# A list scheduler's table of durations and latencies, set from a trace, for a hybrid encoder block

## Chip, cores and metric

One core of a Trainium2 chip runs the whole kernel in one launch. The metric is device time in microseconds of one execution. Engines are named as in the profile: PE (TensorE matmul) and PEld (its weight loads), DVE (VectorE), ACT (ScalarE), POOL (GpSimd), SP (SyncE, which here only issues DMAs).

## What is computed

One layer of an encoder block on x of 1024 positions by 1024 channels, all in float32, cut to its main lines:

```python
h = rms_norm(x, g_mix)
glu_a, glu_b, q, k, v, z, a_in, b_in, gate_a, gate_b = split_cols(h @ w_in, IN_SIZES)
c = depthwise_conv(glu_a * sigmoid(glu_b), conv_dw_w) + conv_dw_b          # 31 taps
y_conv = silu(layer_norm(c, conv_ln_g, conv_ln_b)) @ w_conv_out
q, k, v = split(silu(depthwise_conv([q, k, v], qkv_conv_w)))               # 5 taps
q, k = l2_norm(q) * HEAD_DIM ** -0.5, l2_norm(k)                           # 8 heads of 128
o = gated_delta_rule(q, k, v, g_fwd, beta_fwd) \
    + rev(gated_delta_rule(rev(q), rev(k), rev(v), rev(g_bwd), rev(beta_bwd)))
y_delta = (rms_norm(o, delta_norm_g) * silu(z)) @ w_delta_out
x = x + (sigmoid(gate_a) * y_conv + sigmoid(gate_b) * y_delta) @ w_o
x = x + (silu(gt) * up) @ w_down            # gt, up = split(rms_norm(x, g_ffn) @ w_gate_up)
x = x + sigmoid(rms_norm(x, g_pl) @ w_pl_gate) * rms_norm(p @ w_pl_proj, g_pl_proj)
return rms_norm(x, g_final)
```

The gated delta rule is a recurrence over positions, done in chunks: per chunk a unit lower triangular system is solved, then a chain of small matmuls carries a 128x128 state from chunk to chunk, once forward and once backward.

## The kernel before

**Recorded, then ordered.** The functions in `hybrid_block` do not issue instructions. Each calls a method of the class `Plan` (`matmul`, `transpose`, `act`, `tt`, `stt`, `dma`, ...), which appends an operation with its engine, its tiles and a cost in microseconds. `Plan.order` (line 337) then walks through a modelled time. At each step the engine that is free first takes, of the operations whose inputs are ready and for whose new tiles a buffer is free, the one with the lowest level (a priority by section, in `LV`). An operation ends at its start plus its cost, and one that depends on it on another engine is ready `LAT` later. A DMA takes its issue cost on SP, then at least `DMA_LAT`, then its bytes at `DMA_RATE`, one after the other. `SWITCH` is added where ACT needs another function table. `Plan.run` (line 505) issues everything in the order of the modelled starts. Each engine runs its own instructions in exactly that order and waits on semaphores for the others, so the table of costs decides nothing but the order.

**Products.** A float32 matrix is split into a high and a low part in the type fp32r (`split`: a cast on ACT, a subtraction on DVE), and each product is three matmuls (`mm3`: high by high, high by low, low by high) of 128x128 weights by 512 columns. Some large products use a seven-product scheme for 2x2 blocks. Weights are loaded in pieces of 256 KB into `raw` tiles and split into `w` tiles just before use. The kernel uses eight PSUM tiles of 512 columns, named `ps`.

**Stages.** At the start eight tiles of x are loaded (`big`, 512 KB each), squared and summed on ACT, scaled, transposed on PE and split into `hT`; beside that x itself is transposed and spilled, and eight small vectors are loaded into one tile and transposed. Then the input projection runs block by block (`do_qkv`, `do_glu`, `do_z`, `do_gate`), with the depthwise convolutions as `scalar_tensor_tensor` taps of 128x1024 on DVE. In between, as soon as a pair of heads has its q, k and v, the delta-rule sections run (`group`, `head`): d.np builds the chunk matrices, d.inv and d.lev invert them, d.chain is the recurrence, d.out combines the two directions and normalises. After the last projections come the layer norm and the conv projection (cout), the delta projection (dout), w_o, the feed-forward part and the per-layer embedding.

**Two places in a head.** In d.lev (line 1122 on) the inverses of 32x32 blocks are copied into the tiles `eu` and `et` by 32 copies of 32x128 elements on ACT, then two rounds of matmul, negation of the PSUM bank on ACT (`neg`, into an `m2` tile, shown as `m`) and matmul follow. In d.out two banks of matmuls are added to `o` on DVE; ACT squares eight pieces with a running sum (`sso`); DVE forms the mean square (`rn`, three tiny operations), POOL raises it to the power -1/2, DVE multiplies (`m<-big,rn`), and PE transposes the product:

```python
pn.pow(rn, rn, mhalf16[:, :NJ])
for q4 in range(2):
    on = m2()
    pn.tt(on, o[:, js], rn[:, js, None].spread(4, P), ALU.mult)
    for i in range(4):
        pn.transpose(ps[:, cs(i)], on[:, i], ident)
```

In the profile one line stands for all operations of one helper: L239 matmuls, L244 transposes, L261 plain copies and casts on ACT, L268 other ACT functions, L284 DVE, L312 the power on POOL, L332 DMAs.

## Time and profile before

| what | us |
|---|---|
| median of 3 timed runs | 2121.04 (2121.02 to 2121.16) |
| the profiled execution | 2120.64 |
| its span, first to last instruction | 2118.9 |
| mean granted clock of TensorE | 0.993 |
| data moved by DMA | 292.85 MB, 138 GB/s on the mean |

The profile is of one execution. "Busy" is the time that an engine's own instructions cover; a wait is put down to the instruction whose semaphore came last. PE's matmuls are pipelined, so its busy time tells where it is fed, not that it is at its peak. An instruction in float32 proper (the delta-rule sections, the transposes aside) stands in the trace as two matmul records; one in fp32r has one.

### The profile page before, as it was taken

How to read it: one execution, taken by the hardware profiler on the slowest of the kernel's cores; microseconds unless marked ns; L12 is line 12 of the kernel's file. 1: busy time of each engine (PE TensorE's matmuls, PEld its weight loads, DVE VectorE, ACT ScalarE, POOL GpSimd, SP SyncE). 2: the span in 40 equal slices, each digit the busy share in tenths (PEclk: the TensorE clock that was granted, in tenths of full speed). 3: DMA queues.
4: the chain of work that ended last, by engine and by line, in shares of the span. 5: the costliest groups of instructions: out<-in, count | busy, mean ns of one | idle time of the engine just before them, and what ended most of it. 6: DMA issues, size and time to landing. Idle time of an engine off the chain costs nothing.

```text
span 2118.9 us, 29685 instructions
## 1 busy us (share of the span) xinstructions
PE 2068.0 (98%) x10326; PEld 1714.5 (81%) x10326; DVE 1650.1 (78%) x2696; ACT 1137.0 (54%) x2590; POOL 130.4 (6%) x203
## 2 busy tenths in 40 slices
PE   7999999999999999999999999999999999999998
PEld 5888788878888788878888888888888888777888
DVE  4488999977899989888587977797666657888776
ACT  6636656756657655857886445443333335443542
POOL 1000201110110101111100000000000000000000
PEclk9999999999999999999999999999999999999999
DMA  6334224522323412636468587433323337442253
GB/s 216 106 120 133 80 82 140 185 84 80 128 93 124 149 60 78 211 95 204 153 201 253 185 271 245 144 112 113 100 90 109 100 96 258 153 159 86 63 164 107
DMA packets 296726, 292.85 MB, mean 138 GB/s; under 512 B 17945, under 2 KB 217810, under 8 KB 296576
## 3 DMA queue, kind: packets, MB, share of 16 engines
q1 hardware_dynamic: 296576, 290.95, 42.8%
q8 instruction: 81, 1.33, 0.3%
q14 instruction: 69, 0.57, 0.1%
HBM read 205.10 MB, written 85.79 MB: 137 GB/s over the span
## 4 chain that ended last, share of the span: by engine, by line
PE 84%; ACT 7%; DVE 5%; DMA 2%; issue 1%; SPq 0%; DVEq 0%; POOLq 0%; POOL 0%; ACTq 0%
PE ps L239 82%; ACT big L261 4%; DVE big L284 3%; PE ps L244 2%; DVE mid L284 1%; ACT big L268 1%; ACT m L268 1%; DMA big<-in_x_dram 1%; DVE w L284 1%; ACT w L261 1%; DMA big<-d 1%; DMA d<-mid 0%; SPq L332 0%; ACT mid L268 0%; ACT L268 0%
## 5 line engine op out<-in xcount | busy, mean ns | idle before, releaser
L239 PE MATMUL ps<-big,w 128*128 128x512 f32 (+1 forms) x7416 | 1823.7, 399 | 2.9 <-ACT w L261 1.4
L239 PEld LDWEIGHTS ps<-big,w 128*128 128x128 f32 x7416 | 1362.0, 189 | 303.4 <-ACT w L261 2.4
L284 DVE SCALAR_TENSOR_TENSOR big<-big,cw 128x1024 f32<-128x1024 f32 x336 | 434.3, 1299 | 17.3 <-ACT big L268 12.3
L261 ACT CAST w<-raw 128x512 fp32r<-128x512 f32 (+2 forms) x308 | 184.6, 605 | 274.2 <-PE ps L239 216.0
L284 DVE TENSOR_TENSOR w<-raw,w 128x512 fp32r<-128x512 f32 (+2 forms) x308 | 208.2, 682 | 74.4 <-ACT w L261 72.6
L261 ACT CAST w<-mid 128x512 fp32r<-128x512 f32 (+1 forms) x185 | 107.4, 586 | 166.2 <-PE ps L239 104.5
L284 DVE TENSOR_TENSOR big<-big 128x512 fp32r<-128x512 f32 (+2 forms) x222 | 149.5, 702 | 11.0 <-ACT big L261 7.9
L284 DVE TENSOR_TENSOR w<-mid,w 128x512 fp32r<-128x512 f32 (+1 forms) x185 | 118.4, 644 | 44.8 <-ACT w L261 44.0
L284 DVE TENSOR_TENSOR big<-ps,big 128x512 f32<-128x512 f32 (+1 forms) x146 | 100.3, 688 | 43.1 <-PE ps L239 33.2
L239 PEld LDWEIGHTS ps<-big 128*128 128x128 f32 x784 | 101.9, 195 | 15.7 <-issue 8.8
L239 PE MATMUL ps<-big 128*128 128x128 f32 (+1 forms) x784 | 107.1, 283 | 7.3 <-ACT big L261 5.1
L261 ACT COPY big<-big 32x128 f32<-32x128 f32 (+1 forms) x264 | 102.6, 440 | 16.5 <-DVE big L284 12.6
L261 ACT CAST big<-big 128x512 fp32r<-128x512 f32 x147 | 85.8, 619 | 40.6 <-DVE big L284 24.0
L261 ACT COPY big<-ps 32x128 f32<-32x128 f32 (+3 forms) x162 | 66.8, 413 | 62.2 <-PE ps L239 53.1
L261 ACT COPY mid<-ps 128x512 f32<-128x512 f32 x81 | 47.0, 588 | 70.2 <-PE ps L239 57.4
L244 PE MATMUL ps<-ident,big 128*128 128x128 f32 (+1 forms) x432 | 71.5, 279 | 12.8 <-DMA big<-in_x_dram 8.8
L239 PEld LDWEIGHTS ps<-S,big 128*128 128x128 f32 x448 | 71.8, 190 | 10.0 <-DVE S L284 0.2
L239 PE MATMUL ps<-S,big 128*128 128x128 f32 x448 | 75.0, 275 | 0.0
L239 PEld LDWEIGHTS ps<-big,m 128*128 128x128 f32 x512 | 63.8, 194 | 12.2 <-ACT m L268 9.4
L244 PEld LDWEIGHTS ps<-ident,big 128*128 128x128 f32 (+1 forms) x432 | 53.6, 146 | 23.9 <-issue 12.1
L239 PE MATMUL ps<-big,m 128*128 128x128 f32 x512 | 65.7, 279 | 6.4 <-ACT m L268 6.3
L268 ACT ACTIVATE mid<-mid 128x512 f32<-128x512 f32 (+2 forms) x87 | 50.2, 580 | 37.7 <-DVE mid L284 23.7
(161 smaller groups left out, 1714.7 us busy)
## 6 DMA issues: line engine op xcount, KB each, us to landing
raw<-in_w_in_dram SPq DMA_DIRECT2D x128, 256.0 KB, 3.1
d<-mid SPq DMA_DIRECT2D x120, 256.0 KB, 3.0
mid<-d SPq DMA_DIRECT2D x120, 256.0 KB, 3.2
big<-d SPq DMA_DIRECT2D x119, 256.0 KB, 5.1
d<-big SPq DMA_DIRECT2D x103, 256.0 KB, 2.8
big<-dqkv SPq DMA_DIRECT2D x32, 512.0 KB, 5.1
raw<-in_w_gate_up_dram SPq DMA_DIRECT2D x50, 256.0 KB, 3.1
dqkv<-big SPq DMA_DIRECT2D x24, 512.0 KB, 2.8
```

The lines of the kernel that those rows point to most:

```text
L239: o = self.add("pe", lambda: self.nc.tensor.matmul(out.ap(), lhsT.ap(), rhs.ap(), start=start, stop=stop, **kw), [out], [lhsT, rhs], cost)
L244: self.add("pe", lambda: self.nc.tensor.transpose(out.ap(), in_.ap(), ident.ap()), [out], [in_, ident], 0.107)
L261: return self.nc.scalar.copy(out.ap(), in_.ap())
L268: return self.nc.scalar.activation(out.ap(), in_.ap(), func, **kw)
L284: return getattr(e, name)(**{k: v.ap() if isinstance(v, View) else v for k, v in kw.items()})
```

## The change

The table of costs and latencies that `Plan.order` uses is replaced. No operation is added, removed or changed, and every dependence stays. The core of the diff:

```diff
-SWITCH = 2.0
+SWITCH = 1.42
...
-DMA_LAT, DMA_RATE = 1.6, 300000.0
+DMA_LAT, DMA_RATE = (1.95, 1.1), 300000.0
+
+COLD = 15.0
...
-LAT = {("pe", "act"): 0.20, ("pe", "dve"): 0.20, ("act", "pe"): 0.27, ("act", "dve"): 0.14, ("dve", "pe"): 0.26,
...
+LAT = {("pe", "act"): 0.235, ("pe", "dve"): 0.205, ("act", "pe"): 0.16, ("act", "dve"): 0.13, ("dve", "pe"): 0.18,
...
-            cost = max(0.107, n / 2400 + 0.003)
+            cost = max(0.119, n / 2208 + 0.004)
...
-        cost = (0.051 if in_.buf.pool.space == PSUM else 0.093) + in_.n / 1200
+        ps, rows = in_.buf.pool.space == PSUM, out.p1 - out.p0
+        cost = (0.06 if ps else 0.1) + in_.n / (1200 if out.dims[-1][0] < 16 else 600)
+        if rows < P and out.buf.tag == "big" and in_.n <= 256:
+            cost += 0.16 if not ps else 0.115 if rows == 32 else 0.07
...
-                 [out], [in0, in1], 0.3 + out.n * 0.165)
+                 [out], [in0, in1], 0.5 if out.n == 1 else 1.1 if out.n == 4 else 1.7)
...
+            if e == "pe" and now < COLD:
+                o.cost *= 2
```

`DMA_LAT` is now a pair (loads, stores); matmuls and transposes on PE count double in the first 15 us of the modelled time. Other rows of the table (DVE, its 32x32 transpose, POOL's fill and select, the issue cost of a DMA, the remaining latencies) change in the same manner. Eleven lines are added in all, so in the new file L239 is L243, L244 is L248, L261 is L268, L268 is L275, L284 is L291 and L332 is L340.

What that moves, at two places. First SP's queue at the start, from the first tile of x on: `big<-in_x` is a tile of x, `raw` a piece of a weight, `mid` a small vector, `bc` a row of constants. Before:

```order
L332 DMA big<-in_x_dram 128x1024 x4
L332 DMA raw<-in_w_in_dram 128x4x128
L332 DMA bc<-in_dt_bias_dram 128x16
L332 DMA raw<-in_w_in_dram 128x4x128
L332 DMA mid<-in_conv_dw_b_dram 8x128
L332 DMA mid<-in_conv_ln_g_dram 8x128
L332 DMA mid<-in_conv_ln_b_dram 8x128
L332 DMA mid<-in_g_ffn_dram 8x128
L332 DMA mid<-in_g_pl_dram 8x128
L332 DMA mid<-in_g_pl_proj_dram 8x128
L332 DMA mid<-in_delta_norm_g_dram 1x128
L332 DMA raw<-in_w_in_dram 128x4x128 x2
```

And now, from the same place:

```order
L340 DMA big<-in_x_dram 128x1024 x2
L340 DMA raw<-in_w_in_dram 128x4x128
L340 DMA bc<-in_dt_bias_dram 128x16
L340 DMA raw<-in_w_in_dram 128x4x128
L340 DMA mid<-in_conv_dw_b_dram 8x128
L340 DMA mid<-in_conv_ln_g_dram 8x128
L340 DMA mid<-in_conv_ln_b_dram 8x128
L340 DMA mid<-in_g_ffn_dram 8x128
L340 DMA mid<-in_g_pl_dram 8x128
L340 DMA mid<-in_g_pl_proj_dram 8x128
L340 DMA mid<-in_delta_norm_g_dram 1x128
L340 DMA big<-in_x_dram 128x1024 x2
```

The third and fourth tile of x moved from the front to behind two weight pieces, a row of constants and seven vectors.

Second, the d.out of the third head (near 550 us in the trace of before). On ACT, where `COPY big<-big 32x4x32` are the copies into `eu` and `et` of the next head's d.lev and `m_...,sso` the eight squares; before:

```order
L261 COPY big<-big 32x4x32 x10
L268 ACTIVATE m_4642,sso<-big 128x128
L261 COPY big<-big 32x4x32
L268 ACTIVATE m_4642,sso<-big 128x128 x2
L261 CAST w<-raw 128x512 x2
L268 ACTIVATE m_4642,sso<-big 128x128
L268 ACTIVATE m_4722,sso<-big 128x128 x4
L261 COPY big<-big 32x4x32 x12
```

And now:

```order
L268 COPY big<-big 32x4x32 x3
L275 ACTIVATE m_4698,sso<-big 128x128
L268 COPY big<-big 32x4x32
L275 ACTIVATE m_4698,sso<-big 128x128 x3
L268 COPY big<-big 32x4x32
L275 ACTIVATE m_4775,sso<-big 128x128 x4
L268 COPY big<-big 32x4x32 x12
```

Seven copies left the place ahead of the first square, and two casts of weights the place between the squares, which one more copy took.

On DVE in the same d.out, where the two `big<-ps,big` are the sums onto `o` and `SCALAR_TENSOR_TENSOR big<-big,cw` are convolution taps; before:

```order
L284 TENSOR_TENSOR big<-ps,big 128x512
L284 SCALAR_TENSOR_TENSOR big<-big,cw_606 128x1024
L284 TENSOR_TENSOR big<-ps,big 128x512
L284 TENSOR_TENSOR w<-raw,w 128x512 x2
L284 SCALAR_TENSOR_TENSOR big<-big,cw_606 128x1024
L284 TENSOR_TENSOR rn<-rn,sso 128x8
L284 TENSOR_SCALAR rn<-rn 128x8
L284 SCALAR_TENSOR_TENSOR big<-big,cw_606 128x1024 x2
L284 TENSOR_TENSOR w<-raw,w 128x512
L284 TENSOR_TENSOR m_5176<-big,rn 128x512
```

And now:

```order
L291 TENSOR_TENSOR big<-ps,big 128x512
L291 SCALAR_TENSOR_TENSOR big<-big,cw_421 128x1024
L291 TENSOR_TENSOR big<-ps,big 128x512
L291 SCALAR_TENSOR_TENSOR big<-big,cw_449 128x1024 x2
L291 TENSOR_TENSOR rn<-rn,sso 128x8
L291 TENSOR_SCALAR rn<-rn 128x8
L291 SCALAR_TENSOR_TENSOR big<-big,cw_449 128x1024 x2
L291 TENSOR_TENSOR m_5178<-big,rn 128x512
```

Three subtractions of weight splits left this stretch, and one more tap came in ahead of `rn`.

On PE between the last matmul of that d.out's sums and its transposes of the product (`ps<-ident,m`), before:

```order
L239 MATMUL ps<-big,m_4644 128x128
L239 MATMUL ps<-big,w 128x512 x40
L244 MATMUL ps<-ident,m_5176 128x128 x4
L239 MATMUL ps<-big,w 128x512
L244 MATMUL ps<-ident,m_5186 128x128 x4
```

And now:

```order
L243 MATMUL ps<-big,m_4708 128x128
L243 MATMUL ps<-big,w 128x512 x30
L248 MATMUL ps<-ident,m_5178 128x128 x4
L243 MATMUL ps<-big,w 128x512
L248 MATMUL ps<-ident,m_5184 128x128 x4
```

PE has 30 matmuls of the projections to do there instead of 40. Over the whole program ACT loads a function table 47 times instead of 42, and the last five matmuls of the conv projection moved from ahead of the delta projection's main part to between the w_o matmuls.

24 lines of the change are left out of this document (14 added, 10 removed).

## The prediction

> **What bounds the kernel now.** First the page's head, its list of engines and the chain that ended last.
>
> ```profile
> span 2118.9 us, 29685 instructions
> PE 2068.0 (98%) x10326; PEld 1714.5 (81%) x10326; DVE 1650.1 (78%) x2696; ACT 1137.0 (54%) x2590; POOL 130.4 (6%) x203
> PE 84%; ACT 7%; DVE 5%; DMA 2%; issue 1%; SPq 0%; DVEq 0%; POOLq 0%; POOL 0%; ACTq 0%
> ```
>
> TensorE is busy for 2068.0 of 2118.9 us and carries 84% of the chain. No instruction of it comes or goes, so the order can win at most the 50.9 us in which it is idle, and what it loses at a lower clock. The profiled execution took 2120.64 us, 1.74 more than its span and 0.40 under the median of the three timed runs (2121.04); the sum is made against 2120.64. A measurement of this kernel can tell about 0.2% (4.2 us) from no change.
>
> Next the windows view: start and end of a stretch, its length, then busy time and instructions of PE, weight loads, DVE, ACT, POOL, and PE's granted clock.
>
> ```profile
> 0.00:60.00 60.00, 46.43 (x262) 35.07 (x263) 24.62 (x48) 38.35 (x68) 6.46 (x25) 0.97 0.60 194
> ...
> 240.00:480.00 240.00, 231.54 (x1268) 195.85 (x1267) 208.74 (x330) 155.97 (x423) 31.73 (x47) 0.98 0.37 120
> 480.00:715.00 235.00, 231.11 (x1269) 196.62 (x1268) 203.72 (x327) 150.83 (x409) 26.50 (x42) 0.99 0.34 109
> 715.00:945.00 230.00, 220.86 (x1235) 187.05 (x1234) 201.22 (x323) 141.58 (x413) 28.64 (x35) 1.00 0.37 120
> 945.00:1035.00 90.00, 85.62 (x514) 74.63 (x513) 66.14 (x114) 66.30 (x177) 12.72 (x13) 0.96 0.52 166
> 1035.00:1300.00 265.00, 265.00 (x1246) 218.00 (x1245) 208.15 (x352) 155.99 (x299) 5.85 (x8) 1.00 0.71 227
> 1300.00:1730.00 430.00, 430.00 (x1858) 346.99 (x1857) 296.40 (x459) 163.96 (x279) 2.01 (x2) 1.00 0.37 117
> ```
>
> The idle time lies in two places: 13.6 us in the first 60 us, and 8.46 + 3.89 + 9.14 + 4.38 = 25.9 us from 240 to 1035 us, where the delta-rule heads run between the projections. From 1035 to 1730 PE is never idle: the order moves there too, but that stretch has nothing to give, and it costs nothing as long as the weights stay ahead.
>
> What PE waits for between 60 and 1035 us (waits view: waiter, releaser, total, times, longest):
>
> ```profile
> PE ps L244 <- DVE m L284: 11.2, 5, 3.7
> PE ps L239 <- ACT m L268: 6.3, 5, 2.4
> PE ps L239 <- ACT big L261: 5.1, 3, 3.3
> ```
>
> The first is the end of a head: squares on ACT, a power on POOL, a product into an `m2` tile on DVE, then PE's transposes (section d.out). The third is the start of a head's block inversion: 32 small copies into `eu` and `et` on ACT, then matmuls (d.lev). The second is the negation between two matmuls of d.lev. The windows just behind the longer waits, and one around the longest:
>
> ```profile
> 321.90:325.30 3.40, 2.82 (x8) 1.91 (x8) 1.15 (x3) 3.35 (x5) 0.04 (x2) 0.50 0.22 89
> 475.50:482.30 6.80, 5.50 (x21) 5.05 (x22) 1.71 (x2) 6.69 (x20) 0.10 (x1) 0.50 0.00 0
> 554.00:557.40 3.40, 3.40 (x17) 3.22 (x16) 2.13 (x5) 3.33 (x9) 0.00 (x0) 0.50 0.30 83
> 783.00:790.00 7.00, 3.28 (x24) 2.69 (x22) 3.61 (x7) 6.88 (x20) 1.64 (x1) 1.00 0.14 41
> 1025.00:1031.80 6.80, 6.80 (x29) 6.22 (x28) 2.81 (x7) 2.10 (x6) 1.51 (x1) 0.50 0.33 116
> ```
>
> Four times the clock was granted at 0.50 for 3.4 or 6.8 us, so a wait can cost twice: itself, and half of the PE work behind it.
>
> **The table against the trace.** Busy time and mean of one, from the groups:
>
> ```profile
> L261 ACT COPY big<-big 32x128 f32<-32x128 f32 (+1 forms) x264 | 102.6, 440 | 16.5 <-DVE big L284 12.6 <-POOL big L316 2.4 <-issue 0.2
> L312 POOL TENSOR_TENSOR rn<-rn,mhalf 128x8 f32<-128x8 f32 x8 | 17.9, 2239 | 108.6 <-DVE rn L284 108.6
> L312 POOL TENSOR_TENSOR nrm<-ssk,half 128x8 f32<-128x8 f32 x8 | 13.1, 1640 | 218.9 <-DVE ssk L284 218.9
> L268 ACT ACT_TABLE_LOAD x41 | 52.6, 1283 | 1.1 <-DVE big L284 0.3 <-DVE mid L284 0.2
> ```
>
> The old table gives a 32x128 copy 0.093 + 128/1200 = 0.200 us, the new one 0.367. For 264 of them that is 53 and 97 us, where the chip was busy for 102.6: the old plan left 50 us of ACT's work out, nearly all of it in d.lev. It also held PE too fast: n/2400 + 0.003 = 0.216 us for 512 columns, where the stretch from 1300 to 1730 shows 430/1858 = 0.231; the new 0.236 is near. These two errors pulled in opposite directions: a PE slower than planned gave the other engines slack; late copies used it up in d.lev and d.out, where PE then waited.
>
> **Term 1, the waits of the heads.** One wait, the d.out of a head near 550 us, can be followed through both orders. Timeline rows of PE, ACT, DVE and POOL:
>
> ```profile
> 540.80 9.59 PE L239 MATMUL ps<-big,w 128*128 128x512 f32 x40
> 553.62 0.83 PE L244 MATMUL ps<-ident,m 128*128 128x128 f32 x4 [3.23 <-DVE m L284]
> ...
> 540.74 2.43 ACT L261 COPY big<-big 32x128 f32<-32x128 f32 x6
> 543.18 0.31 ACT L268 ACTIVATE m<-big 128x128 f32<-128x128 f32 x1
> ...
> 544.65 1.12 ACT L261 CAST w<-raw 128x512 fp32r<-128x512 f32 x2
> ...
> 547.06 0.18 ACT L268 ACTIVATION_READ_ACCUMULATOR m<-big 128x1 f32 x1
> ...
> 540.60 0.68 DVE L284 TENSOR_TENSOR big<-ps,big 128x512 f32<-128x512 f32 x1
> ...
> 542.39 0.68 DVE L284 TENSOR_TENSOR big<-ps,big 128x512 f32<-128x512 f32 x1
> ...
> 547.96 2.60 DVE L284 SCALAR_TENSOR_TENSOR big<-big,cw 128x1024 f32<-128x1024 f32 x2
> 552.88 1.29 DVE L284 TENSOR_TENSOR m<-big,rn 128x512 f32<-128x512 f32 x2
> ...
> 548.14 2.60 POOL L312 TENSOR_TENSOR rn<-rn,mhalf 128x8 f32<-128x8 f32 x1 [9.02 <-DVE rn L284]
> ```
>
> The first square had its input at 541.28 but stood behind ten copies of 2.43/6 = 0.405 us until 543.18; the last square ended at 547.24. In the new order three copies stand ahead, and between first and last square two casts (1.12 us) give way to one more copy (0.41). The squares then end up to 1.9 + 0.7 = 2.6 us earlier, at 544.6. DVE, done with the second sum at 543.07, now has two convolution taps (2.60) ahead of the `rn` steps: 545.7, and 0.35 for those: 546.0. The power takes 1.64 to 2.60 (the two groups above): 547.7 to 548.6; the two taps beside it end at 548.7; the product (0.69) is there at 549.4. But PE has only 30 matmuls to do instead of 40: 540.8 + 30 x 9.59/40 = 548.0. So the wait is about 1.4 instead of 3.23, which is 0.43 of it. I apply this 0.43 to the waits of the same making, 11.2 (d.out) and 5.1 (the copies): 16.3 x 0.57 = **9.3 us won**. I leave the 6.3 us of the negations as they are, since their cost changes little in the table (0.478 to 0.487). Bounds: all three rows gone, 22.6 us won; at the other end the ten matmuls less of cover (2.4 us) without the 2.6 us on ACT, which makes this wait 5.6, and over 16.3/3.23 = 5 such waits 12 us lost. I take the middle because ACT's copies, the late part, are what the new table corrects.
>
> The power varies: 2.24 us after taps on DVE, 1.64 in the other group, for one form. The Trainium skill (SBUF — State Buffer, "SBUF: two separate sides") says that GpSimd and a DVE instruction with two SBUF inputs hold a shared port pair exclusively and that the loser blocks for the whole instruction. The trace agrees in that POOL's 2.60 us run lies beside two taps; by this rule the power would always be near 2.60 here, the wait 1.5 and the gain 8.7.
>
> **Term 2, the clock.** The windows at 321.9, 475.5 and 554.0 follow waits of these two kinds. PE was busy 2.82 + 5.50 + 3.40 = 11.7 us in them at half the clock; if waits of 1.4 us no longer bring it down, half of that, **5.9 us**, is won. The window at 1025 follows a negation and stays. Bounds: 0 (others fall instead) to (11.7 + 6.8)/2 = 9.3. The Trainium skill (TensorE: Matmul & The Clock Gate, "Part 1: The HAM clock gate") says the clock falls after at least one idle window of 3.4 us. The trace differs: a wait of 3.7 us near 784 left it at 1.00 and one of 2.4 ended just before the fall at 1025. By the page only the waits of 3.2 and 3.3 come near, and 4.5 us would be won.
>
> **Term 3, the start.** Two rows of the page's DMA issues (count, size, median us to landing), then SP's queue, the landing of the fourth tile of x in the chain, and the first projection matmul:
>
> ```profile
> raw<-in_w_in_dram SPq DMA_DIRECT2D x128, 256.0 KB, 3.1
> ...
> big<-d SPq DMA_DIRECT2D x119, 256.0 KB, 5.1
> ...
> 3.68 1.78 SPq L332 DMA_DIRECT2D big<-in_x_dram  x4
> ...
> 8.67 0.30 SPq L332 DMA_DIRECT2D mid<-in_conv_ln_g_dram  x1
> ...
> 14.94 0.97 SPq L332 DMA_DIRECT2D big<-in_x_dram  x2
> ...
> 5.02 7.20 DMA big<-in_x_dram
> ...
> 18.21 0.44 PE L239 MATMUL ps<-big,mid 128*64 128x512 f32 x1 [0.95 <-ACT big L268]
> ```
>
> Four tiles of x went out from 3.68 to 5.46, and the fourth landed at 12.22. The new order has two there; the third and fourth stand behind two weight loads and all the small vectors. Each of these issues waits for the DMA eight places ahead of it: the vector at 8.67 left when the first tile of x was in. So the third now leaves once both tiles and the two weight loads ahead are in: three more tiles came in between 8.67 and 12.22, 1.18 each, so 8.67 + 1.18 + 2 x 0.59 = 11.0, and the fourth 0.45 later. Landing then takes 3.1 us (a weight load) to 5.0 (the first tile here, 3.68 to 8.67): the first half is complete at 14.6 to 16.5 instead of 12.22, 2.4 to 4.3 us later, and the squares, transposes and the projection at 18.21 shift with it. Against that, the fifth and sixth tiles, now right behind the fourth and two weight loads, leave some 2 us before 14.94, which bounds the loss below at 0. I take **3 us lost**, near the middle of 2.4 to 4.3; PE's idle time of 13.6 us has no other work to hide it.
>
> Costs at nothing: five more table loads (47 for 42) are 5 x 1.283 = 6.4 us on ACT, which is busy 54%; should all of them stand in a head's chain, they cost those 6.4. The last five matmuls of the conv projection now stand about 100 us later, within w_o's; some 27 us of PE work still separate them from the first w_o matmul that needs them, against at most 5.1 us for each of the four DMAs between (the page's slowest row above), 20.4 together, so nothing waits unless SP's queue holds them up by over 6 us.
>
> **Sum:** 2120.64 - 9.3 - 5.9 + 3.0 = **2108.4 us**.
>
> **Rivals.**
> *The gains cancel.* The old plan's PE was 7% too fast, which handed every head slack; the new one takes it back, as the 30 matmuls for 40 show. If cover and chain shrink alike, terms 1 and 2 are 0 and the start costs 0 to 3: 2120.6 to 2123.6. For it: DVE is 87% busy from 240 to 480, so its place in the chain cannot shrink much. Against it: PE's idle time there is put down to ACT's copies by the trace, not to cover.
> *Slower: less cover, late producers.* At d.out PE arrives 2.4 us sooner while the squares still queue behind copies (0.44 us each, still over the table's 0.367). Price 12 us, plus 3 at the start: 2135.6. It decides where the squares end less than about 0.6 us earlier than before. For it: the power still costs up to 2.60 where the table has 1.7. Against: seven copies and two casts really leave the stretch in front of the squares.
> *All waits go*, 22.6 and 9.3, nothing lost at the start: 2088.7. Against: the worked place still waits.
> *The order does not matter*, since PE is 98% busy: within 2 us of 2120.6. The rows are clearly different, so this is part of the first rival.
>
> **How the numbers follow.** Forecast (2100 to 2116.8) 0.52, all or nearly all gone (under 2100) 0.12, cancelled (2116.8 to 2125.3) 0.20, slower 0.16. The range leaves out half of the second case and most of the last: 2095 to 2127. Faster 0.64, same 0.20, slower 0.16.
>
> **What would show it.** In the profile after: PE's idle time from 240 to 1035 near 16 us instead of 25.9; the waits on DVE `m` and on ACT's copies near 7 instead of 16.3, each under 2 us; one or two half-clock windows there instead of four; the first projection matmul near 21 us instead of 18.21; from 1035 to 1730 no idle time. The prediction is wrong if the copies are planned rightly and PE still waits as long for d.out, if the loss at the start is over 6 us, or if idle time appears behind 1035 us.

## Result, and the profile after

The changed kernel takes 2138.2 us (median of 4 runs, 2137.45 to 2139.2) where the kernel before, on the same chip, takes 2121.1: a ratio of 1.0076, 95% interval 1.0063 to 1.0090. The forecast was 2108.4 us and faster; it is slower by 17 us. The profiled execution took 2138.9 us; these are its head and its chain.

```profile
span 2137.2 us, 29674 instructions
PE 2077.7 (97%) x10326; PEld 1707.7 (80%) x10326; DVE 1644.8 (77%) x2696; ACT 1144.3 (54%) x2595; POOL 126.2 (6%) x203
PE 65%; DVE 13%; issue 8%; ACT 7%; DMA 6%; POOL 1%; SPq 1%; DVEq 0%; POOLq 0%; ACTq 0%
```

PE's idle time went from 50.9 to 59.5 us and its busy time for the same instructions from 2068.0 to 2077.7, and the chain now runs through other engines and transfers for a third of the span. The windows view of the changed kernel, at the places shown for before (busy time and instructions of PE, weight loads, DVE, ACT, POOL; then PE's granted clock), tells where:

```profile
0.00:60.00 60.00, 43.66 (x229) 33.45 (x229) 23.42 (x43) 33.52 (x60) 6.86 (x25) 0.91 0.59 190
...
240.00:480.00 240.00, 235.00 (x1288) 197.69 (x1287) 200.36 (x324) 152.15 (x406) 22.57 (x40) 1.00 0.37 120
480.00:715.00 235.00, 231.65 (x1274) 194.87 (x1273) 207.69 (x330) 158.72 (x417) 30.17 (x51) 1.00 0.33 110
715.00:945.00 230.00, 227.87 (x1257) 189.99 (x1256) 210.72 (x335) 144.06 (x407) 27.48 (x34) 1.00 0.39 124
945.00:1035.00 90.00, 87.24 (x523) 74.46 (x521) 68.65 (x116) 73.06 (x198) 13.95 (x16) 1.00 0.49 158
1035.00:1300.00 265.00, 249.70 (x1171) 203.59 (x1172) 191.44 (x327) 145.56 (x288) 6.83 (x8) 0.97 0.68 214
```

From 240 to 1035 us PE's idle time is 5.00 + 3.35 + 2.13 + 2.76 = 13.2 us instead of 25.9, and the clock is full: the heads did what was forecast. But the first 60 us have 16.3 us idle instead of 13.6 and a clock of 0.91, and from 1035 to 1300, where before had no idle time at all, there are now 15.3 us of it.

The waits of the heads, by the groups of PE's matmuls from 240 to 1035 us (busy time, mean ns | idle time before them and its releasers):

```profile
L248 PE MATMUL ps<-ident,m 128*128 128x128 f32 x56 | 8.8, 280 | 2.9 <-DVE m L291 2.7
L243 PE MATMUL ps<-big 128*128 128x128 f32 x452 | 60.4, 276 | 3.0 <-ACT big L268 2.8 <-DVE big L291 0.3
L243 PE MATMUL ps<-big,m 128*128 128x128 f32 x449 | 58.4, 279 | 1.0 <-ACT m L275 0.9
```

The wait for the product of d.out fell from 11.2 to 2.7 us, that for ACT's copies from 5.1 to 2.8, that for the negations from 6.3 to 0.9.

**One yardstick for all runs.** Two orders do not do the same work in the same window, so windows of two runs cannot simply be subtracted. For the table of runs below, every matmul gets one price (0.234 us for 512 columns, near the 0.231 of before's stretch from 1300 to 1730; 0.222 for a float32 pair; 0.111 to 0.119 for the small ones), the prices are added up in PE's order, and the times at which two traces reach the same sum of PE work are compared. Five stages: the start (up to 60 us of PE work, which before reaches 80.8 us into its trace), the heads (to 1050), behind the heads (layer norm, conv projection and delta projection, to 1200), w_o (to 1300), and gate-up, down and the rest. For after against before: **+7.7, -13.1, +5.1, +13.4, +5.2, together +18.3 us**, which is the difference of the spans (2137.2 - 2118.9).

**The start.** SP's queue, PE and the chain of the changed kernel:

```profile
3.63 0.82 SPq L340 DMA_DIRECT2D big<-in_x_dram  x2
...
10.73 0.82 SPq L340 DMA_DIRECT2D big<-in_x_dram  x2
```

```profile
20.79 0.71 PE L243 MATMUL ps<-big,mid 128*64 128x512 f32 x1
...
35.76 1.52 PE L248 MATMUL ps<-ident,big 128*128 128x128 f32 x7 [4.96 <-ACT mid L268]
```

```profile
25.69 0.59 ACT mid L268
26.28 0.02 issue
26.29 8.72 DMA d<-mid
...
35.12 0.59 ACT mid L268
35.71 0.04 issue
35.76 1.31 PE ps L248 x5
```

The third and fourth tile of x leave at 10.73 and the first projection runs at 20.79 instead of 18.21, as worked out (11.0 and about 21). Then something came that was not: a store of a transposed tile of x took 8.72 us to land, where the new table plans 1.1 us and 0.87 for its bytes; the tile that it frees is the next that ACT fills and PE waits for, 4.96 us. The clock stood at one half for 10.24 us, from 35.51 us on. The kernel before has as slow a store, but PE has work beside it and waits for only 1.06 us, with the clock at one half for 3.4 us behind it (chain and PE's row of before):

```profile
35.28 8.84 DMA d<-mid
...
44.85 0.33 PE L244 MATMUL ps<-ident,big 128*128 128x128 f32 x1 [1.06 <-ACT mid L261]
```

So not the store is new, but its place in the order. For the first 60 us of PE work PE's busy time went from 67.2 to 71.5 us and its idle time after its first instruction from 5.0 to 9.2; it begins 0.7 us sooner, which leaves 7.7 lost.

**w_o.** The chain of the changed kernel around 1290 us, and the clock behind it:

```profile
1276.16 0.70 DVE mid L291
...
1276.88 2.08 DMA d<-mid
...
1278.98 2.80 DMA mid<-d
...
1281.81 0.70 DVE mid L291
...
1282.95 3.40 DMA mid<-d
...
1288.81 2.00 DMA d<-mid
...
1290.85 2.69 DMA big<-d
...
1293.57 0.63 ACT big L268
1294.19 0.04 issue
1294.23 2.07 PE ps L243 x4
```

```profile
1279.70 3.42 PE L243 MATMUL ps<-big,w 128*128 128x512 f32 x14
1294.23 6.13 PE L243 MATMUL ps<-big,w 128*128 128x512 f32 x17 [11.11 <-ACT big L268]
```

```profile
1288.20:1298.40 10.20, 4.17 (x10) 3.29 (x11) 3.08 (x5) 2.76 (x5) 0.00 (x0) 0.50 0.66 232
```

The last conv-projection matmuls end at 1276.1. Behind them stands a chain of five transfers one after another, two merges and a split, 18.1 us long. (A merge multiplies a block of the delta projection with its gate and adds the conv projection's block to it.) PE has 7.0 us of other work (up to 1283.1), then waits 11.11 us; the clock goes to one half in the midst of the wait and stays there for 4.2 us of work behind it.

**Behind the heads, and in the down projection.** All of PE's waits for weights that ACT splits (waits view: total, times, longest), the row of the longest, and the clock at two of them:

```profile
PE ps L243 <- ACT w L268: 7.4, 4, 3.9
```

```profile
1923.24 4.99 PE L243 MATMUL ps<-big,w 128*128 128x512 f32 x14 [3.90 <-ACT w L268]
```

```profile
1171.80:1175.20 3.40, 3.40 (x9) 2.68 (x10) 3.40 (x7) 2.18 (x4) 0.00 (x0) 0.55 0.24 89
...
1923.10:1926.50 3.40, 3.26 (x8) 2.58 (x9) 3.17 (x7) 2.18 (x6) 0.00 (x0) 0.50 0.25 64
```

One of the four, of 0.4 us, lies in the heads. Two lie behind them, 0.75 us before 1161.2 and 2.37 before 1171.8; with 3.4 us at half the clock behind the second they make most of the 5.1 us. The longest lies in the down projection and makes, with the half clock at it, the 5.2: ACT could cast that weight only after a subtraction on DVE (1922.04 us), which stood behind a row of splits of other tiles.

### The profile page after: what moved, and what is told of

It is laid out like the page before. It is cut to its first block, busy times and chain, and to the rows that moved or that the text cites. A ratio compares the mean times of both kernels' runs of the same rounds, so it can differ in the third digit from the quotient of the medians.

```text
span 2137.2 us, 29674 instructions
## 1 busy us (share of the span) xinstructions
PE 2077.7 (97%) x10326; PEld 1707.7 (80%) x10326; DVE 1644.8 (77%) x2696; ACT 1144.3 (54%) x2595; POOL 126.2 (6%) x203
## 4 chain that ended last, share of the span: by engine, by line
PE 65%; DVE 13%; issue 8%; ACT 7%; DMA 6%; POOL 1%; SPq 1%; DVEq 0%; POOLq 0%; ACTq 0%
PE ps L243 63%; DVE big L291 9%; ACT big L268 3%; PE ps L248 2%; DVE mid L291 2%; DVE w L291 1%; DMA big<-d 1%; ACT big L275 1%; DMA d<-mid 1%; DMA mid<-d 1%; DMA raw<-in_w_in_dram 1%; ACT w L268 1%; ACT m L275 1%; DMA big<-dqkv 1%; SPq L340 1%
## 5 line engine op out<-in xcount | busy, mean ns | idle before, releaser
L243 PE MATMUL ps<-big,w 128*128 128x512 f32 (+1 forms) x7416 | 1824.8, 400 | 19.4 <-ACT big L268 11.1
L243 PEld LDWEIGHTS ps<-big,w 128*128 128x128 f32 x7416 | 1361.0, 189 | 327.7 <-ACT big L268 11.7
L291 DVE SCALAR_TENSOR_TENSOR big<-big,cw 128x1024 f32<-128x1024 f32 x336 | 433.4, 1294 | 16.4 <-ACT big L275 10.6
L268 ACT CAST w<-raw 128x512 fp32r<-128x512 f32 (+2 forms) x308 | 184.1, 604 | 262.1 <-PE ps L243 202.0
L291 DVE TENSOR_TENSOR w<-raw,w 128x512 fp32r<-128x512 f32 (+2 forms) x308 | 208.7, 681 | 75.7 <-ACT w L268 74.5
L268 ACT CAST w<-mid 128x512 fp32r<-128x512 f32 (+1 forms) x185 | 107.6, 586 | 163.3 <-PE ps L243 113.9
L291 DVE TENSOR_TENSOR big<-big 128x512 fp32r<-128x512 f32 (+2 forms) x222 | 149.4, 702 | 22.9 <-ACT big L268 17.0
L291 DVE TENSOR_TENSOR w<-mid,w 128x512 fp32r<-128x512 f32 (+1 forms) x185 | 118.3, 643 | 54.0 <-ACT w L268 53.5
L291 DVE TENSOR_TENSOR big<-ps,big 128x512 f32<-128x512 f32 (+1 forms) x146 | 100.2, 687 | 45.5 <-PE ps L243 36.4
L268 ACT CAST big<-big 128x512 fp32r<-128x512 f32 x147 | 87.0, 619 | 46.1 <-DMA big<-d 24.5
L268 ACT COPY big<-big 32x128 f32<-32x128 f32 (+1 forms) x264 | 103.5, 441 | 13.4 <-DVE big L291 7.5
L243 PE MATMUL ps<-big 128*128 128x128 f32 (+1 forms) x784 | 103.5, 279 | 4.1 <-ACT big L268 2.8
L243 PEld LDWEIGHTS ps<-big 128*128 128x128 f32 x784 | 98.3, 191 | 11.1 <-issue 5.8
L268 ACT COPY big<-ps 32x128 f32<-32x128 f32 (+3 forms) x162 | 66.6, 412 | 61.3 <-PE ps L243 55.1
L248 PE MATMUL ps<-ident,big 128*128 128x128 f32 (+2 forms) x432 | 75.2, 292 | 20.4 <-DMA big<-in_x_dram 9.4
L275 ACT ACTIVATE mid<-mid 128x512 f32<-128x512 f32 (+2 forms) x87 | 50.2, 584 | 69.1 <-DMA mid<-d 42.8
L248 PEld LDWEIGHTS ps<-ident,big 128*128 128x128 f32 (+2 forms) x432 | 56.6, 153 | 36.4 <-issue 12.1
L268 ACT COPY mid<-ps 128x512 f32<-128x512 f32 x81 | 46.5, 589 | 64.8 <-PE ps L243 54.0
L243 PEld LDWEIGHTS ps<-S,big 128*128 128x128 f32 x448 | 70.9, 190 | 11.8 <-DVE S L291 2.3
L243 PE MATMUL ps<-S,big 128*128 128x128 f32 x448 | 76.0, 275 | 0.2 <-DVE S L291 0.2
L275 ACT ACTIVATE big<-big 128x1024 f32<-128x1024 f32 (+2 forms) x80 | 56.6, 715 | 29.2 <-DVE big L291 21.5
L268 ACT COPY m<-ps 128x512 f32<-128x512 f32 x48 | 28.1, 586 | 77.2 <-PE ps L243 77.2
```

Of the source, the lines that this page charges most:

```text
L243: o = self.add("pe", lambda: self.nc.tensor.matmul(out.ap(), lhsT.ap(), rhs.ap(), start=start, stop=stop, **kw), [out], [lhsT, rhs], cost)
L248: self.add("pe", lambda: self.nc.tensor.transpose(out.ap(), in_.ap(), ident.ap()), [out], [in_, ident], 0.11)
L268: return self.nc.scalar.copy(out.ap(), in_.ap())
L275: return self.nc.scalar.activation(out.ap(), in_.ap(), func, **kw)
L291: return getattr(e, name)(**{k: v.ap() if isinstance(v, View) else v for k, v in kw.items()})
```

## The experiments

Besides the changed kernel 18 others ran, each beside the kernel before on the same chip. This table has all of them: median time, ratio to before with its 95% interval, and by stage what the profiled execution lost (+) or won (-) against that of before, in us at equal PE work.

| run | us | ratio (95%) | start | heads | behind | w_o | gate-up on |
|---|---|---|---|---|---|---|---|
| after | 2138.2 | 1.0076 (1.0063-1.0090) | +7.7 | -13.1 | +5.1 | +13.4 | +5.2 |
| heads | 2128.8 | 1.0036 (1.0022-1.0050) | -0.8 | -9.8 | +18.7 | +0.2 | -0.7 |
| start_old | 2134.4 | 1.0071 (1.0058-1.0084) | -2.0 | -9.7 | +4.3 | +14.1 | +6.0 |
| cout | 2136.8 | 1.0081 (1.0069-1.0094) | +8.1 | -12.8 | +14.1 | +1.9 | +4.9 |
| anull | 2127.5 | 1.0031 (1.0019-1.0043) | +7.3 | -10.3 | +4.2 | +1.8 | +6.2 |
| null1 | 2127.1 | 1.0030 (1.0017-1.0043) | +2.0 | -0.6 | +6.5 | +0.2 | -0.9 |
| null4 | 2131.8 | 1.0049 (1.0034-1.0064) | -1.6 | -1.4 | +13.7 | +0.1 | -0.7 |
| heads_cout | 2123.8 | 1.0013 (1.0003-1.0022) | +0.8 | -8.9 | +13.1 | +0.1 | -0.3 |
| heads_pool | 2135.4 | 1.0072 (1.0055-1.0089) | -0.3 | -9.5 | +23.9 | +0.2 | -0.5 |
| heads_q2 | 2128.3 | 1.0040 (1.0025-1.0055) | +3.8 | -10.2 | +18.7 | +0.2 | +0.1 |
| dma_new | 2136.2 | 1.0075 (1.0060-1.0090) | -1.2 | +0.4 | +7.7 | +0.1 | +4.5 |
| dma_old | 2123.3 | 1.0015 (1.0005-1.0024) | -2.5 | -7.9 | +10.1 | +0.1 | +0.6 |
| dmaold_nocold | 2123.7 | 1.0016 (1.0005-1.0027) | -0.1 | -8.1 | +11.6 | 0.0 | +2.3 |
| dma_28 | 2131.4 | 1.0048 (1.0033-1.0063) | -1.7 | -3.8 | +11.6 | 0.0 | +4.4 |
| dma_30 | 2114.5 | 0.9970 (0.9960-0.9980) | -3.4 | -18.0 | +14.5 | +0.1 | +0.1 |
| dma_32 | 2120.3 | 0.9994 (0.9985-1.0004) | -2.5 | -15.8 | +12.8 | 0.0 | +5.0 |
| dma_40 | 2131.3 | 1.0046 (1.0031-1.0061) | -0.4 | -4.3 | +10.9 | +6.0 | 0.0 |
| splice_a | 2099.8 | 0.9895 (0.9882-0.9909) | -3.4 | -17.3 | -0.1 | +0.1 | -1.0 |
| splice_b | 2135.3 | 1.0057 (1.0044-1.0070) | +1.2 | +0.7 | +12.7 | +0.2 | +0.2 |

How exact a stage is can be read from heads, heads_pool and heads_q2, whose PE orders are the same: within 5 us at the start (-0.8, -0.3, +3.8), within 1 in the heads. Each stage is read from one trace.

### The change in parts of the program: heads, start_old

For these two, an operation carries both prices, and the planner picks the table as it goes:

```diff
+        tab = 0
+        heads = sum(o.sec.startswith('d.') for o in ops)
...
+            tab = int(now >= 55 and heads > 0)      # heads
+            tab = int(now >= 55)                    # start_old
+            o.cost = o.costs[tab]
...
-                s.ready = max(s.ready, o.end + LAT[e, s.eng])
+                s.ready = max(s.ready, o.end + LAT[tab][e, s.eng])
...
             done.append(o)
+            heads -= o.sec.startswith('d.')
```

> Old table up to 55 planned us, new table as long as an instruction of the heads (d. sections) is left, then the old one. Theory (the loss and the gain of the change are separate by stage; the heads gained 13.1 us at equal PE work, the start lost 7.7, the stages behind them 23): near 2121 - 13 = 2108 us, between 2104 and 2112; the first 60 us as before, PE idle near 13 us from 240 to 1035 us instead of 25.9, and no wait of w_o, since the last five conv-projection matmuls are done at some 1126 us of PE work. Rival (any shuffle of the order moves the time by some 10 us either way, the stages do not add up): anywhere from 2110 to 2140, with gains and losses at other places than in the changed kernel.

> Old table up to 55 planned us, the new one from there to the end. The last five conv-projection matmuls still stand behind 1215 us of PE work. Theory (separate stages): 2138.2 - 7.7 = 2130.5 us, between 2127 and 2134, and the wait of about 11 us in w_o is still there. Rival 1 (the loss behind the heads follows from the start): near 2121 or below. Rival 2 (the start loss is only put off, since later work fills it): near 2138.

The start's loss is gone in both (-0.8 and -2.0), and the heads won 9.8 and 9.7 us: these two stages behave as separate parts. But heads did not give 2108: it lost 18.7 us behind the heads, at a place where the changed kernel loses 5.1, and ended at 2128.8. That is the rival's result. start_old came to 2134.4, 0.4 us above its range, with w_o's wait as in the changed kernel (10.92 us, 14.1 lost).

### The five matmuls in front of w_o: cout, anull

```diff
# cout
                 w = load_w(w_conv_out[0], 0, KB, b * P)
+                if h == 1 and b >= KB - 2:
+                    to(0.9, "fill", "cout")
                 ps = block_half(w, lambda k, h: cT[k], h, KB)
# anull
-SWITCH = 1.42
+SWITCH = 1.44
```

> The changed kernel with one edit: the last two output blocks of the conv projection (second half of the rows) get a level ahead of the d.out section, so that their matmuls end at 1126 us of PE work instead of 1217; PE's order is that of the changed kernel up to its place 4979. Theory (w_o waits 11.26 us and its clock falls to one half for 10.24 us because these five matmuls were left to the end and their merge holds up the others): near 2138.2 - 13.3 = 2125 us, between 2121 and 2128; the windows at the start and in the heads as in the changed kernel. Rival (the wait comes from the queue of transfers or the planned latencies of loads and stores, whatever these matmuls do): 2136 to 2140, with a wait of 10 us at the same place.

> The changed kernel with the planned price of a table load on ACT at 1.44 us instead of 1.42, a difference that says nothing about the chip, but which gives another order; in it the last five conv-projection matmuls end at 1138 us of PE work. Theory (the place of these five matmuls is chance, and the table brings heads -13, start +8, the rest a few us): near 2125 us, 2120 to 2129, no long wait in w_o. Rival (the new table as such drives w_o into the wait, the five matmuls are a bystander): 2135 to 2141 with a wait of about 10 us in w_o.

In both the five matmuls stand early and w_o's loss falls from 13.4 to 1.9 and 1.8 us; in start_old they stand late, as in the changed kernel (at 1217 us of PE work), and it is 14.1. In these orders the wait of 11 us belongs to these five. The total is another matter: cout took 2136.8, not 2125, since with the same order of PE up to its place 4979 it lost 14.1 us behind the heads where the changed kernel lost 5.1. anull took 2127.5. A planned price that is 0.02 us higher, which says nothing about the chip, is worth 10 us here.

### How much an order is worth by itself: null1, null4

Before's table, with the price of a table load alone changed (`SWITCH = 2.02` and `SWITCH = 1.95` for 2.0).

> The kernel before with the planned price of a table load on ACT at 2.02 us instead of 2.00: a difference that says nothing about the chip, yet PE's order differs at 1440 places, from its place 1045 on. Theory (the order of before is a lucky one behind the heads: there PE finds the weights of the delta projection ready by 2 us and less, so most other orders lose some us there): 2123 to 2130 us, the loss at 1050 to 1150 us of PE work. Rival (before's order is typical for the old table, and what the changed kernel lost comes from the new numbers): 2118 to 2123.

> The kernel before with the planned price of a table load at 1.95 us instead of 2.00, a second order of the old table beside null1; PE's order is the same at 5624 places. Theory (before's order is the better of many that the old table gives): 2123 to 2133 us, with 4 us or more lost behind the heads, none in w_o, none in gate-up and down. Rival (null1 was an unlucky one): 2117 to 2123.

Both lost, 5.9 and 9.8 us, and nearly all of it behind the heads (6.5 and 13.7). So before's order is not a typical one of its own table: behind the heads it is the best of all orders that ran, and any other that the planner made loses 4 us or more there.

### What paces PE behind the heads: heads_cout, heads_pool, heads_q2

heads_cout is heads with the edit of cout. The other two keep the order of heads and change what an instruction runs on:

```diff
# heads_pool: w - round(w) of the conv and delta projections on POOL
-            e = self.nc.vector if eng == "dve" else self.nc.gpsimd
+            e = self.nc.vector if eng == "dve" and not o.pool else self.nc.gpsimd
...
+            pn.ops[-1].pool = pn.sec in ("cout", "dout")
# heads_q2: their raw weights on POOL's own queue
+        raw = self.sec in ("cout", "dout") and isinstance(out, View) and out.buf.tag == "raw"
-        self.add("sp", lambda: self.nc.sync.dma_start(out=ap(out), in_=ap(in_)),
+        self.add("sp", lambda: (self.nc.gpsimd if raw else self.nc.sync).dma_start(out=ap(out), in_=ap(in_)),
```

> The run heads with the level edit of the run cout; the last conv-projection matmuls end at 1117.8 us of PE work, as in before. The run heads won 10.6 us up to 1050 us of PE work and then lost 18.8 up to 1150, all behind the heads. Theory (that loss hangs on where the last conv-projection blocks stand, which here are as in before): 2121 - 10 = 2111, up to 2116. Rival (what PE wins in the heads it waits for behind them, since the layer norm and the weights there are paced by other engines and by transfers, wherever those blocks stand): 2118 to 2130.

> The run heads in the same planned order, but the second parts of the weights (the difference of a weight and its rounded copy) of the conv and delta projections run on POOL instead of DVE, which takes some 0.6 us for each of about 120 off DVE from 1035 to 1260 us. Theory (DVE paces the weights behind the heads, 18.8 us lost there): at least 6 us of them come back, 2115 to 2123. Rival 1 (transfers pace them): within 3 us of 2128.8. Rival 2 (POOL is slower per weight, over 1.2 us, and PE waits longer for it): over 2131.

> The run heads in the same planned order, but the loads of the raw weights of the conv and delta projections are issued by POOL on a queue of its own, no longer behind SP's other transfers, each of which waits for the one 8 places ahead. Theory (SP's queue paces the weights behind the heads; in the chain of the run heads three loads of w_conv_out take 3.8 to 5.6 us one behind the other from 1110 to 1129 us): at least 6 of the 18.8 us lost there come back, 2115 to 2123. Rival (DVE paces them, or the raw buffers do): within 3 us of 2128.8.

heads_cout has the conv-projection's end where before has it and still loses 13.1: the place of those matmuls is not what costs time in this stage. A second queue changed nothing (18.7 again). POOL for DVE made it worse (23.9). By the groups of heads_pool the step takes more than twice the 0.68 us of DVE:

```profile
L301 POOL TENSOR_TENSOR w<-raw,w 128x512 fp32r<-128x512 f32 x40 | 55.3, 1393 | 82.0 <-ACT w L277 76.0 <-DMA raw<-in_w_conv_out_dram 3.6 <-PE ps L248 2.4
```

PE waits for POOL's weights for 3.4 us in all. The longest wait behind the heads, 3.93 us for a weight that DVE splits, fell to 0.90, but another one, for a `big` tile from DVE, grew from 3.16 to 5.21. So a shorter queue did not help this order, and heads_pool gave no clean answer on DVE, since POOL was the slower engine.

### The table by groups of rows: dma_old, dma_new, dmaold_nocold

dma_old is the changed kernel with the old rows of transfers, dma_new the kernel before with the new ones.

```diff
# dma_old, against after
-DMA_LAT, DMA_RATE = (1.95, 1.1), 300000.0
+DMA_LAT, DMA_RATE = (1.6, 1.6), 300000.0
...
-       ("act", "sp"): 0.1, ("dve", "sp"): 0.11, ("sp", "act"): 0.06, ("sp", "dve"): 0.09, ("sp", "pe"): 0.17,
-       ("sp", "sp"): 0.0}
-LAT = {(a, b): LAT.get((a, b), 0.2) for a in ENGS for b in ENGS}
+LAT = {(a, b): LAT.get((a, b), 0.9 if a == "sp" else 0.2) for a in ENGS for b in ENGS}
...
-                 0.53, nbytes)
+                 0.475, nbytes)
# dmaold_nocold, beside that
-COLD = 15.0
+COLD = 0.0
```

> The changed kernel with the table's transfer rows as before (1.6 us for loads and stores, 0.9 us behind a transfer, 0.475 us per issue), all rows of the engines new. Planned landing of a 256 KB load is then 3.37 us instead of 2.9, of a store that is read back 3.37 instead of 1.97; in the profile of after they take 2.9 to 6.5 (loads) and 2.8 (stores) from 1040 to 1255 us. Theory T (the new transfer rows are too short under load, so the plan sets work behind transfers that are not there yet; the engines' rows are right and win in the heads): start within 3 us of before instead of +7.7, heads still 10 to 13 us won, behind the heads 5 to 10 lost as in any other order, gate-up and down within 1 us of before instead of +5: 2110 to 2122 us. Rival R (the engines' rows lose at the start and in down; transfers are a bystander): 2130 to 2140.

> The kernel before with the new transfer rows alone, all rows of the engines old. Theory T: start 6 to 9 us lost (the third and fourth tile of x stand behind the vectors as in after), nothing won in the heads, 6 to 18 lost behind them, about 5 in gate-up and down: 2135 to 2150 us. Rival R: within 6 us of before, 2115 to 2127.

> The run dma_old without the doubled price of PE's instructions in the first 15 planned us. The first projection matmul stands behind 5.5 us of PE work, as in before, where dma_old has it behind 17. Theory (at the start it is transfers and the place of the first projections that count): the first 60 us as before, within 1 us, and 0 to 3 us better there than dma_old; the rest a draw within 6 us of dma_old. Rival (the doubled price is what keeps PE fed at the start): 2 us or more worse in the first 60 us.

The rows split cleanly in the heads: with the engines' rows new, 7.9 us are won; with the transfers' alone, nothing (+0.4). The other runs agree: in all fourteen whose heads were planned with the engines' new rows the heads won 3.8 to 18.0 us, in null1, null4 and dma_new with the old ones 1.4 at most. How much is won within this range is a draw. dma_old came to 2123.3, 1.3 us above its theory's range. The rows of transfers alone cost 15 us in all (2136.2), as much as the whole change, but not as expected: at the start they lost nothing (-1.2). The start's loss came only with both groups new, and goes with either; what in their interplay makes it was not tried. dmaold_nocold has the first projections early and the start of before (-0.1). That is 2.4 us worse than dma_old, where its rival put 2 or more, but a start is exact to 5 us only: the two runs do not tell what the doubled price of PE's first instructions is worth, and beside the new rows of transfers it was not tried.

Loads do take longer than planned where PE waits. The DMA issues from 1040 to 1255 us (count, size, median us to landing), of after and then of before:

```profile
raw<-in_w_conv_out_dram SPq DMA_DIRECT2D x31, 256.0 KB, 5.2
...
mid<-in_w_delta_out_dram SPq DMA_DIRECT2D x8, 256.0 KB, 6.5
```

```profile
raw<-in_w_conv_out_dram SPq DMA_DIRECT2D x32, 256.0 KB, 3.8
...
mid<-in_w_delta_out_dram SPq DMA_DIRECT2D x8, 256.0 KB, 4.8
```

The new table plans 2.9 us for these. From that came a theory: planned landings that are too short put work behind transfers that are not there yet. Two numbers speak against it from the outset: before's loads take longer than 2.9 us as well and cost PE nothing, and in heads, which lost 18.7 us there, the first row has 4.0.

### Longer planned transfers: dma_30, dma_28, dma_32, dma_40

The changed kernel with `DMA_LAT = (3.0, 2.0)`, and with 2.8, 3.2 and 4.0 for the loads.

> The changed kernel with longer transfers: 3.0 us for loads, 2.0 for stores, so that 256 KB land after 3.9 and 2.9 us, near the 3 to 5 and 2 to 3 us of the profile. Theory T (transfers planned too short are what loses): start within 3 us of before, heads 10 to 13 won, 0 to 8 lost behind them, down within 1: 2108 to 2118 us. Rival (each order is a draw, and before's was a good one, whatever the transfers cost): 2120 to 2132.

> The run dma_30 with 2.8 us for loads instead of 3.0; PE's order is the same at 4924 of 9256 places only. Theory T (longer planned transfers are what helps; dma_30 at 2114.5 us was no single lucky draw): 2110 to 2119 us, start and gate-up and down within 3 us of before. Rival (dma_30 was a lucky draw): 2119 to 2135, with losses behind the heads as in the other runs.

> The run dma_30 with 3.2 us for loads instead of 3.0; PE's order is the same at 5192 places. Theory T: 2110 to 2119 us, as dma_28. Rival (lucky draw): 2119 to 2135.

> The run dma_30 with 4.0 us for loads, so that 256 KB land after 4.9 us, as loads did in the profile of after between 1040 and 1255 us (4.9 to 6.5). Theory T': the 14.6 us that dma_30 lost behind the heads come from loads that still land later than planned (5.1 and 5.9 us in its chain there), so less than 10 are lost there: 2105 to 2115. Rival: the loss there stays at 10 to 19 whatever the planned load: 2113 to 2125.

dma_30 was faster than before, 2114.5 us, and looked like proof. Its neighbours were not: 2131.4 and 2120.3, and 2131.3 with the load about as long as the trace shows it (4.9 us planned), which is above both ranges. The theory fell. Behind the heads all four lost 10.9 to 14.5 whatever the load costs, and in gate-up and down (in the order of the loads' price) 4.4, 0.1, 5.0 and 0.0 follow no rule. In dma_40 the split that w_o waited for in the changed kernel is late again, by 4.2 us, with the five matmuls early (at 1126 us of PE work): they are one way into that wait, not the only one. What dma_30 had was a very good order in the heads (-18.0).

### Two orders put together crosswise: splice_a, splice_b

One question was left: is the time behind the heads lost because the orders there are bad, or because PE arrives sooner than everything else does? Here no scheduler runs; the order is a list of two halves, cut at 1045 us of PE work. PE's order in splice_a is that of dma_30 up to its place 5009 and that of before from its place 4700 on (between the two they are one); splice_b is the reverse.

```diff
     def order(self):
         ops = self.ops
+        return [ops[i] for i in SEQ]
```

> The order of dma_30 up to 1045 us of PE work, from there every instruction that is left in the order of before; no scheduler runs. Up to there dma_30 is 21.4 us ahead of before; behind it dma_30 lost 14.6 and before nothing. Theory O (the loss behind the heads is in the order there, and before's is the good one): 2121 - 21.4 = 2099.6 us, up to 2106. Theory L (the loss is the price of arriving sooner: layer norm, weights and transfers there are not sooner, so PE's lead is eaten in any order): 2110 to 2118, 10 us or more lost between 1050 and 1200 us of PE work.

> The other half: the order of before up to 1045 us of PE work, from there that of dma_30. Theory O: before's time plus the 14.6 us that dma_30's order loses behind the heads, 2130 to 2138 us. Theory L: PE arrives as late as in before, so little is lost: 2118 to 2126.

splice_a took 2099.8 us (2099.6 expected by theory O), splice_b 2135.3. PE arrives 20.8 us sooner in splice_a and loses nothing behind the heads; it arrives as late as ever in splice_b and loses 12.7. The windows view of both (splice_a, then splice_b):

```profile
1035.00:1300.00 265.00, 265.00 (x1198) 216.05 (x1198) 207.86 (x345) 143.52 (x258) 4.01 (x3) 1.00 0.74 235
```

```profile
1035.00:1300.00 265.00, 257.17 (x1200) 209.81 (x1199) 197.80 (x334) 150.70 (x289) 6.18 (x8) 0.98 0.69 218
```

So for these two orders the order behind the heads is the cause, and not PE's earlier arrival. The changed kernel's own order there was not joined to another beginning; that null1, where PE arrives 1.4 us later than in before, loses 6.5 us there and null4, where it arrives 3.0 us sooner, 13.7 speaks for the same cause. One place shows how. A matmul of the delta projection waits 3.94 us in splice_b; PE's row, and DVE's last instructions before it:

```profile
1210.83 24.36 PE L565 MATMUL ps<-big,w 128*128 128x512 f32 x95 [3.94 <-DVE w L610]
```

```profile
1204.10 0.68 DVE L610 TENSOR_TENSOR m<-ps,m 128x512 f32<-128x512 f32 x1
1204.70 0.68 DVE L610 TENSOR_TENSOR mid<-raw,mid 128x512 f32<-128x512 f32 x1
1205.30 0.68 DVE L610 TENSOR_TENSOR mid<-ps,m 128x512 f32<-128x512 f32 x1
...
1209.50 0.68 DVE L610 TENSOR_TENSOR mid<-ps,mid 128x512 f32<-128x512 f32 x1
1210.10 0.68 DVE L610 TENSOR_TENSOR w<-mid,w 128x512 fp32r<-128x512 f32 x1
```

The weight of that matmul begins with the difference at 1204.70, and its last step (1210.10) stands behind eight other instructions of DVE, which is busy without a gap. In splice_a the first and the last of the same three steps (the one between is ACT's) are:

```profile
1165.05 0.68 DVE L610 TENSOR_TENSOR mid<-raw,mid 128x512 f32<-128x512 f32 x1
...
1174.38 0.68 DVE L610 TENSOR_TENSOR w<-mid,w 128x512 fp32r<-128x512 f32 x1
```

with the matmul at 1177.31: begun 12.3 us ahead of it instead of 6.1, and ready 2.3 us early. The instructions are the same in both programs; what differs here is the turn that this weight gets on DVE. A matmul at the same place (1138.4 us of PE work) waits 3.4 to 3.9 us for DVE in eight other runs, in heads, heads_q2, null4, dma_old, dmaold_nocold, dma_28, dma_30 and dma_32, and so under the old table too (null4: 3.94). In the waits view of the whole program it is the longest of its kind (heads, then dma_30):

```profile
PE ps L248 <- DVE w L301: 5.8, 3, 3.9
```

```profile
PE ps L243 <- DVE w L291: 4.8, 4, 3.9
```

splice_a is 22 us faster than before and the fastest that ran: the order of dma_30 to the end of the heads (the engines' rows new, the loads planned longer), before's order behind them.

## Why the prediction was wrong, step by step

- **The table against the trace**, and **term 1, "the waits of the heads", 9.3 us won: right.** Between 60 and 1050 us of PE work the idle time fell from 25.9 to 14.6, 11.3 us. The sum is right partly by luck: the two rows that were priced won 10.8 us (16.3 to 5.5) and the negations, left as they were, 5.4 more (6.3 to 0.9), but 4.9 came back in waits that were not in the sum. dma_new (no gain) and dma_old (7.9) show that the engines' rows did it; how near the size came is luck too, since other orders from these rows won 3.8 to 18.0 us in the heads.
- **Term 2, "the clock", 5.9 us won: right by window, too large in all.** All four half-clock windows went. By the yardstick's prices PE did 9.9 us of work in their 18.6 us of busy time, so half of the busy time was the right price. But PE's busy time for the same work fell by 1.9 us only (1003.4 to 1001.6): outside these windows the work took 6.8 us longer in the new order, and why was not found. Both terms together: 13.1 won for 15.2 forecast.
- **Term 3, "the start", 3 us lost: mis-sized.** Its chain came as worked out, 2.6 us at the first projection. Not priced was the store that holds a buffer: before has it too (8.84 us), but in the new order PE runs out of work beside it; with the half clock behind its wait the start lost 7.7, of which 4.3 are longer busy time. heads and start_old show that it goes with the old table's first 55 us.
- **"Costs at nothing ... some 27 us of PE work still separate them from the first w_o matmul that needs them": this step failed, 13.4 us.** The five matmuls belong to the second half of the rows, and the 27 us are the cover of w_o's second half. But a merge takes both of the two `mg` tiles, which go round in a fixed turn, and a merge of the first half stands behind theirs; what w_o needs first, a tile of the first half, is 7.0 us of PE work away, and the chain is 18.1 us long. cout, anull and start_old tie the wait to these matmuls; in dma_40 the same split is late (4.2 us) without them.
- **"From 1035 to 1730 PE is never idle ... that stretch has nothing to give, and it costs nothing as long as the weights stay ahead": this failed too, 5.1 us, and more in most other orders.** No idle time meant no slack: every order from the planner other than before's lost 4 to 19 us there. splice_a and splice_b show for two orders that the order there, not PE's earlier arrival, is what costs.
- **Gate-up and down, +5.2 us: never priced.** Seven runs lost 4.4 to 6.2 us there, and all seven at one place: the matmul at 1844.9 us of PE work waits 3.4 to 4.3 us for ACT's cast of a weight, and at its end the clock goes to one half, for 3.4 us (dma_32: 6.8). Five of them have the new rows of transfers to the end; dma_28 and dma_32 have longer loads, but dma_30, between the two, lost 0.1. The seven with the old rows in that stage lost at most 0.6 (dmaold_nocold, with the old rows as well, 2.3). So the wait is known, but no single row is shown to be what brings this turn about; that stays open.
- **Together:** 2.1 short in the heads, 4.7 more at the start, 13.4 in w_o, 5.1 behind the heads and 5.2 in the rest are the 30.5 us between the forecast and the profiled execution.
- **The rivals.** The slower one had the right side for the wrong reason: d.out's wait fell, and that its 2135.6 us is near the 2138.2 is luck. None named the true mechanism, a new order that takes a stage without idle time out of its fit. Two of the listed signs of a wrong prediction came about: over 6 us lost at the start, and idle time behind 1035 us.

## What to carry to other kernels

A scheduler's table that fits the trace better does not make a better schedule by itself: a small change of any price draws a new order, and in a program that is 98% busy on one engine a draw was worth 6 to 17 us here, as much as the correction. A stage without idle time is a stage that a new order can only harm; price it by the shortest cover of what moves, along every buffer that it passes in turn. Once the gain and the loss are known by stage, keep the good half of each order: the two halves joined won 22 us where the table alone lost 17.

## What the runs showed of the hardware

- The granted clock is 1.00 or 0.50 in every trace here. In the changed kernel it stood at 0.50 for 10.24 us at the waits of 4.96 and 11.11 us and for 3.4 at those of 2.37 and 3.90; in the kernel before for 3.4 or 6.8. The Trainium skill (TensorE: Matmul & The Clock Gate, "Part 1: The HAM clock gate") gives a free-running window of 3.41 us; the trace agrees in the lengths, 3.4 us and two and three times that. At 0.50 PE takes almost twice as long: 18.6 us busy for 9.9 us of work in the four windows of before's heads, 10.0 for 5.7 in the 10.24 us at the start of the changed kernel.
- The landing of one 256 KB transfer ranges from 2.0 us (a store at w_o) to 8.72 and 8.84 us (stores at the start), with medians of 3.8 and 4.8 us (before) and 5.2 and 6.5 us (after) for weights between 1040 and 1255 us, where the DMA engines are 68 and 70% busy. No single latency fits.
- The time of one and the same order varies more than the first runs showed: before took 2117.5 to 2124.4 us in 24 runs on one chip and 2119.1 to 2128.1 in 11 on another, where the first three lay within 0.14 us.
